# Attention scores of two heads in the two row halves of TensorE's array, three products instead of four, and two heads' queries turned by one transpose

## The chip, the cores and the metric

The kernel runs on one core of one Trainium2 chip, in one launch. The metric is the device time of the whole program in microseconds (us). Before the change it is 1516.78 us, the median of 3 runs (1512.79 to 1517.85).

## What is computed

One encoder layer over two sequences of 512 tokens with 1024 features: a state-space branch (S5) and a windowed attention branch, gated and merged, and then a squared-ReLU MLP. The change is in the attention branch. It has 16 query heads of 64 features, 4 key/value heads (so 4 query heads share one key head), blocks of 128 tokens, and each query block sees its own and its two neighbouring key blocks:

```python
q = rms_norm(q.reshape(bsz, seq_len, N_HEADS, HEAD_DIM), q_gain)
k = rms_norm(k.reshape(bsz, seq_len, N_KV_HEADS, HEAD_DIM), k_gain)
...
s = jnp.einsum('nqkgd,njkd->nkgqj', qb, kw).astype(jnp.float32) * scale + bias
s = jnp.where(mask[:, None, None], s, NEG_INF)
...
p = jax.nn.softmax(jnp.concatenate([s, sink_col], axis=-1), axis=-1)[..., :-1]
o = jnp.einsum('nkgqj,njkd->nqkgd', p.astype(vs.dtype), vw)
```

## The kernel before, in words

**Precision by parts.** Matmuls run in fp32r. To come near fp32, an operand is held as a high part (rounded to fp32r) and a low part (what the rounding left), and a product a*b is the sum of matmuls over the parts: high*high, high*low, low*high. In most places of this kernel that is three matmuls (`mm3`, L114 to L118).

**The attention stage** (in the trace about 418 to 692 us) goes through 8 steps: for each of the 4 key heads j, the two sequences sq. A step has 4 units, one for each query block qb of 128 tokens. A unit (class `Unit`, L805) treats the 4 query heads of its key head at once: scores (`scores`, L819), the bias and the row maximum on VectorE (`largest`, L825, printed as L827), the exponential on ScalarE (`exp`, L831), turning the probabilities on TensorE (`turn`, L836, printed L839), splitting them into parts (`high` on ScalarE L843, `low` on VectorE L848), the product with the values (`value`, L851, printed L855) and adding the two halves of the result (`lower_part` L859 on ScalarE, `add` L865 on VectorE). A unit with a middle query block has 3 key blocks (384 score columns), one at the end of a sequence 2 (256 columns): 16 units of each kind.

**Queries.** While a step's units run, the query projection of the next step is made, one block of 128 tokens in each unit (class `Tile`, L759): 24 matmuls of 256 columns (`project`, L772), squares and the norm factor (`square` on ScalarE, `power` on VectorE and GpSimd), scaling (`norm`, L789), four transposes, one for each head (`turn`, L794), and the split: the high part on ScalarE (`high`, L799) goes to partitions 0 to 63 and the low part on VectorE (`low`, L802) to partitions 64 to 127. So for each head the high part lies above the low part on the contraction axis. The keys lie twice, in both halves of the partitions (`key_copies`, `key_turn`), as a high tile `kh` and a low tile `kl`. One score matmul with all 128 rows against `kh` gives high*high + low*high, one against `kl` gives high*low + low*low: two matmuls a head, four products.

**The order.** In this stage the order of the instructions on TensorE, ScalarE, VectorE and GpSimd is written out by hand (`manual_schedule`, L973): the loop body L979 to L1073 is the order in each engine's queue, and each engine takes its queue in order. In one turn of the loop stand the scores and exponentials of the current unit `cur`, the turning, splitting and value products of the unit before it (`prev`), the final `add` of the one before that (`owed`), the projection of the next step's block (`new`), the turn and split of the block projected in the turn before (`rows`), pieces of weight to be split (`extra`: the cast on ScalarE when it is popped, the rest on VectorE when `lower()` is called), and once in a step the division by the sums (`div`, `late`) and the next step's keys. SyncE's queue is not written by hand here.

**PSUM.** Scores use the pool `ps_s` with 2 buffers of one bank, turned probabilities and keys `ps_t` with 2, projections and turned queries `ps_acc` with 3, the value product `ps_o` with 1.

**Another place that the prediction reads.** In the state-space part, `lags` (L453 to L462) writes two halves of PSUM's partitions with matmuls of a 64-column stationary operand, alternating between the halves:

```python
for e in range(2):
    gk = e * SH + g
    PE.matmul(ps[e * 64:(e + 1) * 64, g * 144:(g + 1) * 144], lbt[:, ri, q * SG + gk, :],
              ctab[:, gk, ri].rearrange("p n c -> p (n c)"),
              start=ri == 0, stop=ri == 1)
```

Of the kernel before, what the change touches and what calls it, by code (L numbers as in the profile page):

```python
# [12 lines left out]
F32 = mybir.dt.float32  # L13
F32R = mybir.dt.float32r
I32 = mybir.dt.int32
AF = mybir.ActivationFunctionType
# [3 lines left out]
P = 128  # L20
# [7 lines left out]
CB = 256  # L28
N_HEADS = 16
N_KV = 4  # L30
G = 4
# [32 lines left out]
def hybrid_layer(ctx, tc, x, rel, onehot, w_qkv, w_ug, vectors, lam, coefs, w_glu, w_out, ln2,  # L64
                 w_up, w_down, out):
    nc = tc.nc
    V, S, PE, GP, SP = nc.vector, nc.scalar, nc.tensor, nc.gpsimd, nc.sync
# [18 lines left out]
    def sps():  # L86
        return ps_s.tile([P, 512], F32, tag="sps", name="sps")
# [16 lines left out]
    ident = const.tile([P, P], F32, name="ident")  # L104
# [5 lines left out]
    bglu_sb, gain_q, gain_k, nsink = [vec[:, a:b] for a, b in ((0, 8), (8, 9), (9, 10), (10, 26))]  # L110
# [160 lines left out]
    with tc.tile_pool(name="xin", bufs=1, reuse_waits="tile") as xin, tc.tile_pool(name="ssmc", bufs=1) as sc:  # L271
# [146 lines left out]
        ps = ps_o.tile([P, 512], F32, tag="po", name="line")  # L418
# [276 lines left out]
    with tc.tile_pool(name="att", bufs=2, reuse_waits="tile") as ap, tc.tile_pool(name="attc", bufs=1, reuse_waits="tile") as ac:  # L695
# [63 lines left out]
        class Tile:  # L759
# [30 lines left out]

            def turn(self):
                self.pt = self.pt or acc()
                for h in range(G):
                    PE.transpose(self.pt[0:64, h * P:(h + 1) * P], self.qn[:, h], ident)  # L794

            def high(self):
                self.ptv = self.pt[0:64].rearrange("p (h t) -> p h t", h=G)
                self.dst = queries[self.key][:, :, self.t * P:(self.t + 1) * P]
                S.activation(self.dst[0:64], self.ptv, AF.Copy, scale=gain_q[0:64])  # L799

            def low(self):
                V.scalar_tensor_tensor(self.dst[64:128], self.ptv, gain_q[0:64], self.dst[0:64].bitcast(F32),  # L802
                                       op0=ALU.mult, op1=ALU.subtract)

        class Unit:  # L805
# [10 lines left out]
                self.nmx = small.tile([P, G], F32, tag="nmx", name="nmx")  # L816
                self.s, self.pt, self.hl = {}, {}, {}

            def scores(self, h):  # L819
                ps = self.s[h] = sps()  # L820
                qs = queries[self.j, self.sq][:, h, self.qb * P:(self.qb + 1) * P]
                for i, kk in enumerate(keys[self.j, self.sq]):
                    PE.matmul(ps[:, 0:self.nk], qs, kk[:, self.k0 * P:self.k1 * P], start=i == 0, stop=i == 1)  # L823

            def largest(self, h):  # L825
                hh, b0 = self.j * G + h, (self.k0 - self.qb + 1) * P
# [146 lines left out]
        with tc.manual_schedule(engines={ET.PE, ET.Activation, ET.DVE, ET.Pool}):  # L973
            for i, (j, sq) in enumerate(steps):
                nxt = steps[i + 1] if i + 1 < len(steps) else None
                sums = small.tile([P, G, NB], F32, tag="sm", name="sm", bufs=2)
                ya = ap.tile([P, 2, HALF], F32, tag="ya", name="ya")
                extra = pieces_of(i)
                for qb in range(NB):  # L979
                    if 1 <= i < 5:  # L980
                        e, t = divmod((i - 1) * NB + qb, T)
                        GP.dma_start(y2_scr[e, :, :, t, :].rearrange("g c k -> c g k"), y_scr[e, t])
                    if i == 7 and qb == 0:
                        load_gates(0)
                    for m in {6: (qb,), 7: ((4, 5), (6,), (7,), ())[qb]}.get(i, ()):
                        load_y(m)
                    cur = Unit(j, sq, qb, sums, ya)
                    n3 = prev.nkb if prev else 0
                    div = Divide(*steps[i - 1], *done) if qb == 1 and i > 0 else None
                    new = Tile(*nxt, qb) if nxt else None  # L990
                    project = new.project if new else lambda n: glu_pull(n // 2)
                    kd = None
                    if rows and not nxt:
                        rows.pt = acc()
                    if rows and not rows.qn:
                        rows.power()
                    cur.scores(0)
                    cur.largest(0)
                    if qb == 3 and late:
                        late.multiply()  # L1000
                    cur.scores(1)
                    if owed:
                        owed.add()
                    cur.largest(1)
                    if n3:
                        prev.turn(0)
                        prev.high(0)
                    project(6)
                    if n3:
                        prev.low(0)  # L1010
                    cur.exp(0)
                    cur.exp(1)
                    if rows and not rows.qn:
                        rows.norm()
                    if qb == 0 and nxt:
                        kd = key_copies(*nxt)
                    if div:
                        div.invert()
                    cur.scores(2)
                    cur.largest(2)  # L1020
                    if n3:
                        prev.turn(1)
                        prev.high(1)
                    project(4)
                    if n3:
                        prev.value(0, 0)
                    project(2)
                    cur.exp(2)
                    cur.scores(3)
                    if lower:  # L1030
                        lower()
                        lower = None
                    if n3:
                        prev.low(1)
                        prev.value(0, 1)
                    cur.largest(3)
                    if rows:
                        rows.turn()
                    if n3 > 2:
                        prev.turn(2)  # L1040
                    if kd:
                        key_turn(*nxt, kd)
                    if div:
                        div.turn()
                    project(4)
                    if rows:
                        rows.high()
                        rows.low()
                    if n3 > 2:
                        prev.high(2)  # L1050
                    if n3:
                        prev.value(1, 0)
                    cur.exp(3)
                    if n3 > 2:
                        prev.low(2)
                    project(4)
                    if n3:
                        prev.value(1, 1)
                    project(4)
                    if n3 > 2:  # L1060
                        prev.value(2, 0)
                        prev.value(2, 1)
                    if new:
                        new.square()
                    if n3:
                        prev.lower_part()
                    if extra:
                        lower = extra.pop(0)()
                    if qb == 1:
                        late = div  # L1070
                    owed, prev, rows = prev, cur, new
                    if nxt and qb == NB - 1 and sq == 1:
                        load_biases(nxt[0])  # L1073
                done = sums, ya
# [7 lines left out]
            for k in range(prev.nkb):  # L1082
                prev.value(k, 0)
                prev.value(k, 1)
            lower()
            prev.lower_part()
            prev.add()
            div = Divide(*steps[-1], *done, True)
# [461 lines left out]
```

## Time and profile before

| | |
|---|---|
| median of 3 runs | 1516.78 us (1512.79 to 1517.85) |
| the profiled execution | 1514.28 us, its span 1512.5 us |
| TensorE (PE) busy in the span | 96% |
| VectorE (DVE) busy | 74% |
| ScalarE (ACT) busy | 51% |
| mean granted TensorE clock | 0.992 |

The profile comes from one execution. PE is the matmul, PEld the weight load that belongs to it and overlaps the matmuls. Matmuls are pipelined: the duration of one (0.28 us for 256 columns) is longer than the distance at which the next one starts (0.12 us), so a share of busy time near 100% does not say that the array streams all the time. The rate is read from starts that follow each other. "L827" is line 827 of the kernel. In a row of instructions, `out<-in` gives the names of the tiles, `128*64` the rows and columns of the stationary operand, `128x256` the moving operand; in brackets or behind the last bar stands the idle time of the engine before them and what ended it.

### The profile page before, as it was taken

How to read it: one execution, taken by the hardware profiler on the slowest of the kernel's cores; microseconds unless marked ns; L12 is line 12 of the kernel's file. 1: busy time of each engine (PE TensorE's matmuls, PEld its weight loads, DVE VectorE, ACT ScalarE, POOL GpSimd, SP SyncE). 2: the span in 40 equal slices, each digit the busy share in tenths (PEclk: the TensorE clock that was granted, in tenths of full speed). 3: DMA queues.
4: the chain of work that ended last, by engine and by line, in shares of the span. 5: the costliest groups of instructions: out<-in, count | busy, mean ns of one | idle time of the engine just before them, and what ended most of it. 6: DMA issues, size and time to landing. Idle time of an engine off the chain costs nothing.

```text
span 1512.5 us, 21630 instructions
## 1 busy us (share of the span) xinstructions
PE 1458.2 (96%) x7818; PEld 1238.1 (82%) x7818; DVE 1117.1 (74%) x2015; ACT 764.8 (51%) x1362; POOL 192.2 (13%) x360
## 2 busy tenths in 40 slices
PE   6999999999999999997999989999999999999998
PEld 4788888878899998985787878888888888888787
DVE  7998859977646899886985468777777588575653
ACT  6777762235536787784343245555544443433332
POOL 3133351002231333220100000000000000000000
PEclk9999999999999999998999999999999999999999
DMA  4444459229831445273545235444443694454331
GB/s 172 139 167 166 159 168 368 106 86 348 298 124 32 144 120 161 90 276 119 204 170 176 91 112 174 153 151 151 152 153 125 243 359 150 153 181 153 123 123 62
DMA packets 102139, 249.65 MB, mean 165 GB/s; under 512 B 12266, under 2 KB 23786, under 8 KB 102032
## 3 DMA queue, kind: packets, MB, share of 16 engines
q1 hardware_dynamic: 58352, 135.88, 27.6%
q0 software_dynamic: 18048, 57.72, 11.1%
q10 hardware_dynamic: 25632, 54.67, 9.6%
q8 instruction: 62, 1.02, 0.3%
q14 instruction: 45, 0.37, 0.1%
HBM read 173.74 MB, written 90.21 MB: 175 GB/s over the span
## 4 chain that ended last, share of the span: by engine, by line
PE 78%; DVE 9%; ACT 4%; DMA 4%; issue 4%; POOL 1%; ACTq 0%; SPq 0%; DVEq 0%; POOLq 0%
PE acc L185 14%; PE bank L117 13%; PE bank L118 13%; PE bank L116 13%; PE acc L123 5%; PE acc L772 3%; PE acc L117 2%; PE acc L118 2%; PE acc L116 2%; PE po L855 2%; PE sps L547 2%; DVE pl L848 1%; PE sps L823 1%; PE tps L839 1%; DVE p L827 1%
## 5 line engine op out<-in xcount | busy, mean ns | idle before, releaser
L185 PE MATMUL acc<-act,c_hi 128*128 128x512 f32 x768 | 248.8, 399 | 1.0 <-DVE act L304 1.0
L117 PE MATMUL bank<-b_lo,a_hi 128*128 128x512 f32 x448 | 174.5, 390 | 1.1 <-DVE b_lo L1419 1.1
L118 PE MATMUL bank<-b_hi,a_lo 128*128 128x512 f32 x448 | 174.3, 389 | 0.0
L116 PE MATMUL bank<-b_hi,a_hi 128*128 128x512 f32 x448 | 173.5, 389 | 0.0
L185 PEld LDWEIGHTS acc<-act,c_hi 128*128 128x128 f32 x768 | 142.0, 189 | 29.8 <-DVE act L304 2.4
L185 PE MATMUL acc<-act,c_lo 128*128 128x512 f32 x384 | 152.3, 397 | 0.0
L1418 ACT CAST a_hi<-d_a 128x1024 fp32r<-128x1024 f32 x56 | 59.0, 1054 | 179.1 <-PE bank L117 175.7
L116 PE MATMUL bank<-act,act 128*128 128x512 f32 x368 | 144.3, 392 | 4.9 <-ACT act L1308 4.9
L118 PE MATMUL bank<-act,act 128*128 128x512 f32 x368 | 144.2, 392 | 0.0
L117 PE MATMUL bank<-act,act 128*128 128x512 f32 x368 | 144.1, 392 | 0.0
L1419 DVE TENSOR_TENSOR a_lo<-d_a,a_hi 128x1024 fp32r<-128x1024 f32 x56 | 68.5, 1223 | 100.2 <-ACT a_hi L1418 100.2
L772 PE MATMUL acc<-w_hi,act 128*128 128x256 f32 x512 | 116.2, 295 | 0.0
L117 PEld LDWEIGHTS bank<-b_lo,a_hi 128*128 128x128 f32 x448 | 84.1, 188 | 19.3 <-DVE b_lo L1419 1.9
L118 PEld LDWEIGHTS bank<-b_hi,a_lo 128*128 128x128 f32 x448 | 84.1, 188 | 17.5
L116 PEld LDWEIGHTS bank<-b_hi,a_hi 128*128 128x128 f32 x448 | 84.1, 188 | 17.3
L123 PE MATMUL acc<-act,gc_hi 128*128 128x512 f32 x256 | 84.3, 408 | 13.3 <-ACT ga L1133 10.7
L772 PEld LDWEIGHTS acc<-w_hi,act 128*128 128x128 f32 x512 | 87.0, 189 | 3.7
L116 PEld LDWEIGHTS bank<-act,act 128*128 128x128 f32 x368 | 69.8, 190 | 19.8 <-ACT act L1308 5.3
L185 PEld LDWEIGHTS acc<-act,c_lo 128*128 128x128 f32 x384 | 72.4, 189 | 14.1 <-DVE c_lo L176 0.5
L833 ACT ACTIVATE p<-p,nmx 128x257 f32<-128x257 f32 (+1 forms) x128 | 72.2, 564 | 21.9 <-DVE nmx L827 20.3
L118 PEld LDWEIGHTS bank<-act,act 128*128 128x128 f32 x368 | 69.6, 189 | 14.9 <-DVE act L1309 0.4
L117 PEld LDWEIGHTS bank<-act,act 128*128 128x128 f32 x368 | 69.7, 189 | 14.4
(327 smaller groups left out, 3440.3 us busy)
## 6 DMA issues: line engine op xcount, KB each, us to landing
d_a<-a_scr SPq DMA_DIRECT2D x56, 512.0 KB, 3.6
u_raw<-in_w_up_dram SPq DMA_DIRECT2D x32, 512.0 KB, 5.1
a_scr<-t ACTq DMA_DIRECT2D x64, 256.0 KB, 4.9
k<-in_w_down_dram SPq DMA_DIRECT2D x32, 512.0 KB, 6.0
c_raw<-in_w_ug_dram SPq DMA_DIRECT2D x48, 256.0 KB, 3.7
a_scr<-a ACTq DMA_DIRECT2D x46, 256.0 KB, 2.0
ct_scr<-ctab POOLq DMA_DIRECT2D x16, 576.0 KB, 3.5
ctab_in<-ct_scr POOLq DMA_DIRECT2D x16, 576.0 KB, 7.6
```

The costliest lines, as they stand in the source:

```text
L116: PE.matmul(ps, a[0], b[0], start=first, stop=False)
L117: PE.matmul(ps, a[0], b[1], start=False, stop=False)
L118: PE.matmul(ps, a[1], b[0], start=False, stop=last)
L123: PE.matmul(ps, w[wi][:, k, :], rows[yi], start=k + p == 0, stop=k == KT - 1 and p == 2)
L185: PE.matmul(ps, w[wi][:, k, :], hT[s][hi][:, k, :], start=n == 0, stop=n == 3 * KT - 1)
L547: PE.matmul(ps[:, i * P:(i + 1) * P], bm[:, ri, g, :], u_sb[:, gp * SH + g, :], start=True, stop=True)
L772: PE.matmul(self.ps, hT[sq][act][:, k, col:col + P], w[:, k % 4, :], start=i == 0, stop=i == 3 * KT - 1)
L823: PE.matmul(ps[:, 0:self.nk], qs, kk[:, self.k0 * P:self.k1 * P], start=i == 0, stop=i == 1)
L833: S.activation(p, p, AF.Exp, bias=self.nmx[:, h:h + 1], scale=-1.0, accum_out=self.sums[:, h, self.qb:self.qb + 1])
L855: PE.matmul(self.po, vv, self.hl[i][part], start=i + part == 0, stop=i == self.nkb - 1 and part == 1)
L1418: S.copy(hi, src)
L1419: V.tensor_sub(lo, src, hi.bitcast(F32))
```

## The change

Three things are changed together.

- `Tile.turn` makes two transposes of 128 x 128 instead of four of 128 x 64: two heads stand above each other after the turn. `high` and `low` then work on 128 partitions x 256 elements instead of 64 x 512. In the tile of queries the first index is now the part (high or low) and the pair m of heads, and the partitions hold the two heads of a pair.
- `Unit.scores` takes a pair of heads. Each head has the 64 rows of its half of the array, and three products are made (high*high, high*low, low*high; low*low is left out): 6 matmuls of 64 rows for two heads, alternating between the halves, into the two score banks. Before, there were 4 matmuls of 128 rows for two heads.
- The order of the unit is rewritten: the scores stand at two places of a unit instead of four, the projection goes in pieces of 8, 4, 4, 4 and 4 instead of 6, 4, 2, 4, 4 and 4, and `exp(2)`, `low(1)`, `low(2)`, `rows.low()`, the cast of a weight piece and its `lower()` move.

```diff
             def turn(self):
                 self.pt = self.pt or acc()
-                for h in range(G):
-                    PE.transpose(self.pt[0:64, h * P:(h + 1) * P], self.qn[:, h], ident)
+                for m in range(2):
+                    PE.transpose(self.pt[:, m * P:(m + 1) * P],
+                                 self.qn[:, 2 * m:2 * m + 2].rearrange("p e d -> p (e d)"), ident)
 
             def high(self):
-                self.ptv = self.pt[0:64].rearrange("p (h t) -> p h t", h=G)
-                self.dst = queries[self.key][:, :, self.t * P:(self.t + 1) * P]
-                S.activation(self.dst[0:64], self.ptv, AF.Copy, scale=gain_q[0:64])
+                self.ptv = self.pt[:, 0:CB].rearrange("p (m t) -> p m t", m=2)
+                self.dst = [queries[self.key][:, n * 2:n * 2 + 2, self.t * P:(self.t + 1) * P] for n in range(2)]
+                S.activation(self.dst[0], self.ptv, AF.Copy, scale=gain_q)
 
             def low(self):
-                V.scalar_tensor_tensor(self.dst[64:128], self.ptv, gain_q[0:64], self.dst[0:64].bitcast(F32),
+                V.scalar_tensor_tensor(self.dst[1], self.ptv, gain_q, self.dst[0].bitcast(F32),
                                        op0=ALU.mult, op1=ALU.subtract)
...
-            def scores(self, h):
-                ps = self.s[h] = sps()
-                qs = queries[self.j, self.sq][:, h, self.qb * P:(self.qb + 1) * P]
-                for i, kk in enumerate(keys[self.j, self.sq]):
-                    PE.matmul(ps[:, 0:self.nk], qs, kk[:, self.k0 * P:self.k1 * P], start=i == 0, stop=i == 1)
+            def scores(self, m):
+                self.s[2 * m], self.s[2 * m + 1] = sps(), sps()
+                qs = queries[self.j, self.sq][:, :, self.qb * P:(self.qb + 1) * P]
+                for n, (a, b) in enumerate(((0, 0), (0, 1), (1, 0))):
+                    for e in range(2):
+                        rows = slice(e * 64, (e + 1) * 64)
+                        PE.matmul(self.s[2 * m + e][:, 0:self.nk], qs[rows, a * 2 + m],
+                                  keys[self.j, self.sq][b][rows, self.k0 * P:self.k1 * P], start=n == 0, stop=n == 2)
...
                     cur.largest(0)
                     if qb == 3 and late:
                         late.multiply()
-                    cur.scores(1)
+                    cur.largest(1)
                     if owed:
                         owed.add()
-                    cur.largest(1)
                     if n3:
                         prev.turn(0)
                         prev.high(0)
-                    project(6)
+                    project(8)
                     if n3:
                         prev.low(0)
                     cur.exp(0)
...
-                    cur.scores(2)
-                    cur.largest(2)
                     if n3:
                         prev.turn(1)
                         prev.high(1)
+                    if extra:
+                        lower = extra.pop(0)()
                     project(4)
                     if n3:
                         prev.value(0, 0)
-                    project(2)
-                    cur.exp(2)
-                    cur.scores(3)
-                    if lower:
-                        lower()
-                        lower = None
+                    cur.scores(1)
+                    cur.largest(2)
                     if n3:
-                        prev.low(1)
                         prev.value(0, 1)
-                    cur.largest(3)
                     if rows:
                         rows.turn()
                     if n3 > 2:
...
+                    cur.largest(3)
                     project(4)
                     if rows:
                         rows.high()
-                        rows.low()
+                    if n3:
+                        prev.low(1)
                     if n3 > 2:
                         prev.high(2)
+                        prev.low(2)
+                    if rows:
+                        rows.low()
                     if n3:
                         prev.value(1, 0)
+                    cur.exp(2)
                     cur.exp(3)
-                    if n3 > 2:
-                        prev.low(2)
                     project(4)
...
                     if n3:
                         prev.lower_part()
-                    if extra:
-                        lower = extra.pop(0)()
+                    if lower:
+                        lower()
+                        lower = None
```

After the loop, one `lower()` that was left over goes.

More of the change, by code (lines that the diff above doesn't have):

```diff
@@ L1084, in hybrid_layer @@
                 prev.value(k, 1)
-            lower()
             prev.lower_part()
```

## The prediction

> **What bounds the kernel now.** I read the page first, for the whole program.
>
> ```profile
> PE 1458.2 (96%) x7818; PEld 1238.1 (82%) x7818; DVE 1117.1 (74%) x2015; ACT 764.8 (51%) x1362; POOL 192.2 (13%) x360
> ```
>
> TensorE carries the program; the other engines have room on the average. That average says little about one stage, so next I took the busy time by stretches: the four lead-in tiles and the values' projection, then the loop with the units.
>
> ```profile
> core 0: us, PE busy (x) PEld busy (x) DVE busy (x) ACT busy (x) POOL busy (x), PEclk, DMA share, GB/s
> 415.00:465.00 50.00, 48.31 (x403) 47.90 (x402) 18.67 (x39) 13.61 (x30) 13.17 (x22) 1.00 0.28 98
> 465.00:692.00 227.00, 222.45 (x1596) 203.78 (x1595) 201.02 (x518) 179.19 (x453) 59.84 (x111) 1.00 0.45 143
> ```
>
> In the loop (227 us, 32 units, 7.1 us each, full clock) VectorE is busy 201 us, almost as much as TensorE. So I need TensorE's own stream without its waits. The groups of TensorE by form in 465 to 692 us give the counts:
>
> ```profile
> L772 PE MATMUL acc<-w_hi,act 128*128 128x256 f32 x448 | 104.0, 297 | 0.0
> L772 PE MATMUL acc<-w_lo,act 128*128 128x256 f32 x224 | 63.0, 281 | 0.0
> L839 PE MATMUL tps<-ident,p 128*128 128x128 f32 x312 | 46.7, 272 | 0.0
> L855 PE MATMUL po<-pl,va 128*128 128x512 f32 x77 | 32.9, 427 | 3.7 <-DVE pl L848 3.0
> L855 PE MATMUL po<-ph,va 128*128 128x512 f32 x77 | 31.0, 403 | 0.5 <-DVE ya L865 0.3
> L823 PE MATMUL sps<-kh,qa 128*128 128x384 f32 x64 | 21.7, 340 | 0.3 <-DVE nmx L827 0.3
> L823 PE MATMUL sps<-kl,qa 128*128 128x384 f32 x64 | 21.6, 338 | 0.0
> L794 PE MATMUL acc<-ident,qn 128*64 128x128 f32 x116 | 17.5, 273 | 0.0
> L823 PE MATMUL sps<-kl,qa 128*128 128x256 f32 x64 | 17.4, 282 | 0.0
> L823 PE MATMUL sps<-kh,qa 128*128 128x256 f32 x64 | 17.3, 281 | 0.0
> L123 PE MATMUL acc<-act,gc_hi 128*128 128x512 f32 x31 | 11.3, 427 | 0.0
> ```
>
> Their mean durations are latencies; what one costs in a stream is the distance from start to start, from TensorE's timeline (two stretches of the loop; first the start in us, then the length):
>
> ```profile
> 505.55 0.34 PE L823 MATMUL sps<-kh,qa 128*128 128x384 f32 x1
> 505.73 0.34 PE L823 MATMUL sps<-kl,qa 128*128 128x384 f32 x1
> 505.90 0.34 PE L823 MATMUL sps<-kh,qa 128*128 128x384 f32 x1
> 506.07 0.33 PE L823 MATMUL sps<-kl,qa 128*128 128x384 f32 x1
> 506.25 0.60 PE L839 MATMUL tps<-ident,p 128*128 128x128 f32 x4
> ...
> 521.51 0.28 PE L823 MATMUL sps<-kh,qa 128*128 128x256 f32 x1
> 521.63 0.28 PE L823 MATMUL sps<-kl,qa 128*128 128x256 f32 x1
> ```
>
> A third stretch, from the state-space part, has 512 columns (L185), and between them the matmuls of `lags` (L459), to which I come back:
>
> ```profile
> 66.62 0.61 PE L185 MATMUL acc<-act,c_hi 128*128 128x512 f32 x2
> 67.08 0.39 PE L185 MATMUL acc<-act,c_lo 128*128 128x512 f32 x1
> 67.39 1.20 PE L459 MATMUL lag<-ctab,lbt 128*64 128x144 f32 x16
> 68.42 1.15 PE L459 MATMUL sps<-ctab,lbt 128*64 128x144 f32 x16
> 69.50 0.73 PE L185 MATMUL acc<-act,c_hi 128*128 128x512 f32 x2
> 70.08 0.39 PE L185 MATMUL acc<-act,c_lo 128*128 128x512 f32 x1
> ```
>
> 384 columns cost (506.25 - 505.55)/4 = 0.175 us, 256 columns 0.12. Four transposes span 0.60 at 0.272 each, so one follows another after (0.60 - 0.272)/3 = 0.109. 512 columns cost (67.08 - 66.62)/2 = 0.23. The stream is then 672 x 0.12 (L772) + 312 x 0.109 (L839) + 154 x 0.23 (L855) + 128 x 0.175 + 128 x 0.12 (L823) + 116 x 0.109 (L794) + 31 x 0.23 (L123) = 207 us, and some 8 us of smaller groups that I do not list: 215 of 227 us, 6.7 us a unit. TensorE bounds the loop, and some 12 us are stalls. What ends most of them is in the waits of its weight loads in the same window (us in total, times, the longest):
>
> ```profile
> PEld po L855 <- DVE pl L848: 9.0, 21, 0.8
> ```
>
> The value product waits for VectorE's low part. A piece of VectorE's timeline in a unit with three key blocks shows why:
>
> ```profile
> 506.60 0.61 DVE L827 CUSTOM_DVE_ANT_0 p<-sps,bias,vec 128x384 f32<-128x384 f32 x1
> ...
> 511.87 0.74 DVE L802 SCALAR_TENSOR_TENSOR qa<-acc,vec,qa 64x512 fp32r<-64x512 f32 x1
> 512.64 0.69 DVE L848 TENSOR_TENSOR pl<-tps,ph 128x512 fp32r<-128x512 f32 x1
> ```
>
> From the first maximum to the end of the last `pl` VectorE needs 6.7 us in its queue, and `rows.low()` (0.74) stands ahead of that `pl`.
>
> **The change part by part.** *Transposes of queries:* two of 0.109 go in each of 32 tiles (28 in the loop, 4 in the lead-in, where TensorE is busy 48.3 of 50 us): -7.0 us, all on TensorE's stream.
>
> *Split of queries:* the same elements lie in 128 partitions x 256 instead of 64 x 512.
>
> ```profile
> L789 DVE TENSOR_TENSOR qn<-acc,rq 128x256 f32<-128x256 f32 x28 | 11.6, 413 | 0.0
> ```
>
> By L789's 0.413 (the nearest row of that size, also read from PSUM) `low` falls from 0.74 by 0.33: VectorE -9 us over 28 units, to about 192. `high` on ScalarE gets shorter likewise. Neither is on TensorE's stream; they count through the stalls.
>
> *Scores:* a pair of heads had 4 matmuls, and gets 6 of 64 rows in 3 pairs. No row shows matmuls in two row halves. The nearest shows two column halves, `lags` at L459, between full matmuls of L185, in the third stretch above. One fp32 matmul of 144 columns alone would cost 0.109 x 144/128 = 0.123, and 32 of them 3.9 us; the 32 took from 67.39 to 69.50, 2.1 us. So two halves run side by side, the weight loads too, and a pair costs one. For the scores I take the same: 3 x 0.175 instead of 4 x 0.175 for the 32 pairs of heads with 384 columns (-5.6 us), 3 x 0.12 instead of 4 x 0.12 for the 32 with 256 (-3.8): -9.4 us. The other bound is two halves one after the other, 6 streams for 4: +18.9.
>
> *Going in and out of the halves.* From 67.08 to 70.08 stand 3.00 us. Three full matmuls are 0.69 and 16 pairs of 0.123 are 1.97. The rest, 0.34 us, is what one excursion costs: a gap of 0.08 before the first half, about 0.1 before the first full matmul, and weight loads that could not be made ahead. There are two excursions a unit, 64 in all: with this price +21.8 us. The bounds are 0 and 0.34 (a gain is out, since every change of shape in these rows costs something or nothing); nothing in the trace shows row halves, and I take 0.34 because it is the only change of shape of this kind that the trace has. The Trainium skill has a rule that speaks against the change here, "TensorEngine Tiling (Array Packing)", section Key Properties: a change of the tiling mode, unlike a change between tiles of one mode, drains the engine. By it the row halves pay as the column halves do; were it true of column halves alone, the sum would be 21.8 us lower. The trace agrees for columns (the 0.34), and no run here shows it for rows.
>
> *Stalls.* Scores at two places need both banks of `ps_s` at once: `scores(1)` waits for `largest(0)` and `largest(1)`. TensorE has until then turn(0), project(8), turn(1), project(4) and one value product, 4 x 0.109 + 8 x 0.12 + 4 x 0.109 + 4 x 0.12 + 0.23 = 2.5 us; VectorE needs two L827 of at most 0.61 plus small reads. That wait is covered. The cast of a weight piece moves ahead by half a unit, with `rows.high`, `high(2)` and the exponentials behind it in ScalarE's queue; its load is on SyncE, whose queue the change does not touch, and its buffer comes free with the `lower()` two pieces back, more than a unit before.
>
> ```profile
> L730 ACT CAST w_hi<-w_raw 128x512 fp32r<-128x512 f32 x12 | 7.4, 619 | 0.0
> ```
>
> Twelve casts waited for nothing before, and half a unit (3.5 us) is little against the 7.1 us that lie between two pieces, so I take none; if a load should be late, ScalarE's tail (below) is what it costs. The waits on `pl` get shorter: ahead of the last `low` no longer stand `rows.low()` (0.74) and the `lower()` of a weight piece, so it lands 0.7 us or more earlier in VectorE's queue; the longest of the old waits was 0.8. `lower()` now stands at the unit's end, with `power` and the next `largest` queued behind it, and scores of the next unit need only the two maxima already done. With the excursions TensorE has (215 - 9.4 - 6.1 + 21.8)/32 = 6.9 us a unit, VectorE 192/32 = 6.0: slack 0.9 instead of 0.4. I take 8 of the 12 us of stalls as gone; the bounds are 0 and 12.
>
> *Sum*, against the profiled execution (1514.28 us, 1.8 over its span, and 2.5 under the median of the runs): 1514.3 - 7.0 - 9.4 + 21.8 - 8.0 = 1511.7 us. A difference of 0.3%, 4.5 us, is about what a measurement of this kernel can tell from no change; this sum is 2.6 below and so within it.
>
> **The rivals.** *Cheap excursions.* Row halves may need less than the 0.34: the trace's row is for column halves in fp32 and a stationary operand of 64 columns, the scores are row halves in fp32r with 128. At 0 the stream is (215 - 15.5)/32 = 6.2 a unit, hardly above VectorE's 6.0, so no stall goes: 1497.9. At 0.17 it is 10.9 us of excursions and perhaps 3 us of stalls gone: 1505.8. Middle 1502. For it: nothing measured; against it: the one row.
>
> *Halves that do not overlap* (the change does not do what it says). Then 64 groups cost 6 streams: 1514.3 - 7.0 + 18.9 = 1526.2 without excursions, and with them and some 10 us of stalls gone 1538. It decides if the second matmul of a pair starts a stream (0.12 or 0.175) after the first. Against it: L459 ran two at a time. For it: in L459 the halves write different partitions, here two matmuls write the same partitions of two banks.
>
> *ScalarE's tail.* `exp(2)` and `exp(3)` now come after the last `high`, and `square` and `lower_part` behind them.
>
> ```profile
> L843 ACT CAST ph<-tps 128x512 fp32r<-128x512 f32 x78 | 44.9, 575 | 5.4 <-PE tps L839 4.8
> L833 ACT ACTIVATE p<-p,nmx 128x385 f32<-128x385 f32 x64 | 39.6, 618 | 9.4 <-DVE nmx L827 8.1
> ...
> L778 ACT ACTIVATE sq<-acc 128x256 f32<-128x256 f32 x28 | 10.6, 380 | 6.5 <-PE acc L772 5.8
> ```
>
> `rows.high` (by L778's size 0.38), `high(2)` 0.575, two exponentials of 0.618 and `square` 0.38 are 2.6 us. They can begin when `rows.turn` is out, 0.7 us after `scores(1)` (0.23 of a value product, two transposes, 0.27 until the last is in), and end 3.3 after it. TensorE has 5 value products, 6 transposes and 12 projections until the next scores, 1.15 + 0.65 + 1.44 = 3.2. `power` at the head of VectorE's next turn waits for `square`, with the next `largest` behind it. So the two are even, and a delay of 0.3 (half an L827 ahead of `exp(3)`) would be paid in 28 units: +8.4, 1520.1. Against it: VectorE's slack of 0.9 above, which can take the delay up.
>
> **How the numbers follow.** Forecast 0.44, cheap excursions 0.31, halves one after the other 0.11, ScalarE's tail 0.14. The forecast's own range is 1507.7 (all stalls gone) to 1519.7 (none gone). Faster by over 0.3% (below 1509.7): all of the cheap excursions and 0.13 of the forecast, 0.44. Slower (above 1518.9): 0.11, 0.11 of the tail, 0.05 of the forecast, 0.27. Within: 0.29. The range 1499 to 1524 leaves out the cheapest excursions and the serial halves, together less than 0.2.
>
> **What would show it.** The two matmuls of a pair at L823's successor should start within 0.01 us of each other, and three pairs of 384 columns take 0.53. The first full matmul behind a group should start some 0.2 us late and the group's first some 0.1; if both gaps are missing, the cheap case is right. The waits on `pl` should fall from 9.0 to about 3. L794 should count 56 in the loop, VectorE's busy time there fall to about 192 us. I am wrong if the pair's starts lie 0.12 apart, if VectorE waits on `square` in most units, or if the loop's length leaves 217 to 230 us.

## The result and the profile after

The changed kernel takes 1531.22 us (median of 4 runs, 1527.91 to 1533.02) against 1516.51 before (4 runs): a ratio of 1.0101, 95% interval 1.0083 to 1.0119. It is slower by 14.7 us, above the range of the forecast (1499 to 1524). The profiled executions differ by 1526.1 - 1512.5 = 13.6 us of span.

The time came in the attention loop: from the first score matmul of its first unit to that of its last lie 220.5 us before (465.4 to 685.8) and 234.3 after (463.8 to 698.1), 13.8 more. Its busy times, over a stretch that is 13 us longer than before's because the loop is:

```profile
core 0: us, PE busy (x) PEld busy (x) DVE busy (x) ACT busy (x) POOL busy (x), PEclk, DMA share, GB/s
465.00:705.00 240.00, 227.10 (x1654) 187.23 (x1653) 194.13 (x518) 170.92 (x453) 59.49 (x111) 1.00 0.42 136
```

VectorE fell from 201 to 194 us and ScalarE from 179 to 171, as the split on all 128 partitions should do; the clock is full. The split itself, `low` on VectorE and `high` on ScalarE, which took 0.745 and 0.672 us before:

```profile
L803 DVE SCALAR_TENSOR_TENSOR qa<-acc,vec,qa 128x256 fp32r<-128x256 f32 x29 | 13.8, 476 | 0.0
```

```profile
L800 ACT ACTIVATE qa<-acc,vec 128x256 fp32r<-128x256 f32 x29 | 13.6, 470 | 19.1 <-PE acc L794 19.1
```

So the engines have less to do and the loop is longer.

The scores, first. The groups of TensorE in the loop (window 465 to 710 us), and then its timeline around one group of a unit with two key blocks:

```profile
L826 PE MATMUL sps<-kh,qa 64*128 64x384 f32 x128 | 25.4, 386 | 0.8 <-DVE nmx L831 0.8
L826 PE MATMUL sps<-kh,qa 64*128 64x256 f32 x124 | 19.2, 329 | 0.0
...
L794 PE MATMUL acc<-ident,qn 128*128 128x128 f32 x58 | 11.1, 273 | 0.0
```

```profile
525.62 0.40 PE L859 MATMUL po<-ph,va 128*128 128x512 f32 x1
525.95 0.39 PE L826 MATMUL sps<-kh,qa 64*128 64x256 f32 x2
526.18 0.28 PE L826 MATMUL sps<-kl,qa 64*128 64x256 f32 x2
526.29 0.28 PE L826 MATMUL sps<-kh,qa 64*128 64x256 f32 x2
526.50 0.50 PE L859 MATMUL po<-pl,va 128*128 128x512 f32 x1
526.84 0.38 PE L794 MATMUL acc<-ident,qn 128*128 128x128 f32 x2
```

The stationary operand is now 64*128: row halves. Each row holds a pair (x2) in the time of one matmul: from the second pair to the third it is 0.11 to 0.12 us, the distance of full matmuls of 256 columns before. And the excursion is there. The value product at 525.62 streams 0.23, so the next matmul could start at 525.85; the first pair starts at 525.95 (0.10 late), the second 0.23 after it instead of 0.12 (0.11 late), the third pair's stream ends at 526.41 and the next full matmul starts at 526.50 (0.09 late), and the one behind it 0.34 later instead of 0.23 (0.11 late): 0.41 us. Where four transposes follow, the last term is smaller and the sum 0.35. The weight loads show the same from their side; in the loop they now stand idle before the scores 47 times, while the profile shows nothing that they wait for:

```profile
PEld sps L826 <- issue: 13.9, 47, 0.4
```

Then the waits of TensorE's matmuls in the loop (window 465 to 707 us): us in total, times and the longest.

```profile
PE po L859 <- DVE pl L852: 8.5, 7, 1.4
PE po L859 <- DVE ya L869: 3.7, 7, 0.5
```

Six of the seven waits for a low part are of 1.38 to 1.39 us, each in the first unit of a step; the seventh is of 0.16. The place, in TensorE's timeline and in VectorE's:

```profile
528.56 0.28 PE L772 MATMUL acc<-w_lo,act 128*128 128x256 f32 x1
530.23 0.51 PE L859 MATMUL po<-pl,va 128*128 128x512 f32 x1 [1.38 <-DVE pl L852]
```

```profile
527.02 0.08 DVE L831 DVE_READ_ACCUMULATOR2_ANT nmx<- 128x1 f32 x1
528.42 0.75 DVE L756 SCALAR_TENSOR_TENSOR kl<-tps,vec,kh 128x512 fp32r<-128x512 f32 x1 [1.32 <-ACT kh L755]
529.09 0.47 DVE L831 CUSTOM_DVE_ANT_0 p<-sps,bias,vec 128x256 f32<-128x256 f32 x1
529.49 0.08 DVE L831 DVE_READ_ACCUMULATOR2_ANT nmx<- 128x1 f32 x1
529.49 0.68 DVE L852 TENSOR_TENSOR pl<-tps,ph 128x512 fp32r<-128x512 f32 x1
```

This is the first unit of a step, in which the next step's keys are turned. VectorE stands idle for 1.32 us at `kl` (L756), which needs ScalarE's `kh`; behind `kl` in its queue are `largest(3)` and `low(1)`, whose result TensorE needs at once. In the old order VectorE waited for `kh` at this place too (6.6 us in seven times, against 9.5 now), but `low(1)` and `largest(3)` stood ahead of `key_turn`.

### The profile page after: what moved, and what is told of

The parts are those of the page before. It is cut to its first block, busy times and chain, and to the rows that moved or that the text cites. A ratio compares the mean times of both kernels' runs of the same rounds, so it can differ in the third digit from the quotient of the medians.

```text
span 1526.1 us, 21733 instructions
## 1 busy us (share of the span) xinstructions
PE 1464.3 (96%) x7882; PEld 1222.7 (80%) x7882; DVE 1109.6 (73%) x2015; ACT 755.2 (49%) x1362; POOL 192.6 (13%) x360
## 4 chain that ended last, share of the span: by engine, by line
PE 83%; DVE 6%; ACT 4%; DMA 4%; issue 3%; POOL 1%; ACTq 0%; SPq 0%; DVEq 0%; POOLq 0%
PE acc L185 13%; PE bank L117 13%; PE bank L118 13%; PE bank L116 13%; PE acc L772 5%; PE acc L123 4%; PE po L859 3%; PE sps L826 3%; PE acc L117 2%; PE acc L118 2%; PE acc L116 2%; PE tps L843 2%; PE sps L547 2%; DMA w_raw<-in_w_out_dram 1%; DMA toep<-toep_scr 1%
## 5 line engine op out<-in xcount | busy, mean ns | idle before, releaser
L772 PE MATMUL acc<-w_hi,act 128*128 128x256 f32 x512 | 111.8, 296 | 0.0
L831 DVE CUSTOM_DVE_ANT_0 p<-sps,bias,vec 128x256 f32<-128x256 f32 (+1 forms) x128 | 66.3, 548 | 17.8 <-PE sps L826 17.3
```

Of the source, the lines that this page charges most:

```text
L772: PE.matmul(self.ps, hT[sq][act][:, k, col:col + P], w[:, k % 4, :], start=i == 0, stop=i == 3 * KT - 1)
L831: V.tensor_tensor_reduce(self.p[:, h, 1:1 + self.nk], self.s[h][:, 0:self.nk], biases[self.j][h][:, b0:b0 + self.nk], -1.0, nsink[:, hh:hh ...
```

## The experiments

The theory after the result (A): the excursions cost what the forecast took, and a new wait in the first unit of a step brings some 11 us. Its rivals: the excursions cost much more and carry it all (B); scores of two heads at one place starve VectorE, whatever the order (C).

The table reads each run's trace: the distance from one unit's first score matmul to the next unit's, mean over the steps, for the four units of a step (units 1 and 4 have two key blocks). Each ratio is against the kernel before, run beside it.

| run | unit 1 | unit 2 | unit 3 | unit 4 | us, median | ratio (95%) |
|---|---|---|---|---|---|---|
| before | 6.20 | 6.64 | 7.96 | 7.72 | 1516.51 | |
| the change | 7.73 | 7.11 | 7.55 | 7.88 | 1531.22 | 1.0101 (1.0083 to 1.0119) |
| e1_low1_ahead | 6.49 | 6.99 | 7.55 | 7.88 | 1520.27 | 1.0018 (1.0009 to 1.0028) |
| e2_old_order | 7.03 | 7.56 | 8.46 | 9.91 | 1552.97 | 1.0234 (1.0219 to 1.0249) |
| e3_twice_out | 8.57 | 7.93 | 8.41 | 8.68 | 1557.45 | 1.0264 (1.0249 to 1.0279) |
| e4_order_alone | 7.45 | 6.78 | 7.47 | 7.58 | 1521.86 | 1.0032 (1.0022 to 1.0042) |
| e5_pair_turn | 5.98 | 6.93 | 8.45 | 8.15 | 1522.94 | 1.0050 (1.0033 to 1.0067) |
| e6_order_low1 | 6.21 | 7.07 | 7.47 | 7.59 | 1516.81 | 1.0000 (0.9989 to 1.0011) |
| e7_order_pair_turn | 6.26 | 7.39 | 7.83 | 8.10 | 1522.93 | 1.0056 (1.0035 to 1.0078) |
| e8_multiply_later | 7.11 | 7.39 | 7.83 | 7.11 | 1524.45 | 1.0051 (1.0035 to 1.0067) |
| e9_one_excursion | 6.19 | 7.05 | 7.55 | 7.92 | 1518.93 | 1.0011 (1.0001 to 1.0021) |
| e10_gp_multiply | 6.26 | 7.06 | 7.55 | 6.94 | 1510.53 | 0.9963 (0.9948 to 0.9978) |
| e11_before_gp | 6.20 | 6.64 | 7.96 | 6.96 | 1511.18 | 0.9965 (0.9953 to 0.9977) |
| e12_mended_gp | 6.49 | 6.99 | 7.55 | 7.24 | 1514.21 | 0.9991 (0.9982 to 1.0000) |

### The low part ahead of the keys

On the changed kernel:

```diff
+                    cur.largest(3)
+                    if n3:
+                        prev.low(1)
                     if kd:
                         key_turn(*nxt, kd)
                     if div:
                         div.turn()
-                    cur.largest(3)
                     project(4)
                     if rows:
                         rows.high()
-                    if n3:
-                        prev.low(1)
```

> The changed kernel with one step of VectorE's queue moved: largest(3) and prev.low(1) stand ahead of the next step's key_turn, whose low part kl (L756) waits for ScalarE's kh. Only the first unit of a step is touched. Theory A (64 excursions at 0.34 to 0.40 us, and a new wait in the first unit of a step, where low(1) stands behind kl, about 1.5 us in 7 units): 10 to 12 us faster than the changed kernel, 1519 to 1522, some 0.3% over before. Theory B (the excursions alone cost more than that and carry the whole 14.7 us; the wait is only a shadow of them): no change, 1529 to 1532.

Measured: 1520.27 us, 10.9 under the changed kernel. Unit 1 fell from 7.73 to 6.49 and no other unit by more than 0.12. As A has it, and against B: about three quarters of the loss stood in one place of VectorE's queue. The edit moves `largest(3)` together with `low(1)`, and no run has one without the other; the wait on TensorE that went is the one for `low(1)`. Of the waits of TensorE's matmuls one kind is left:

```profile
PE po L859 <- DVE ya L869: 3.6, 7, 0.5
```

### The new scores in the old order

The changed kernel's queries and scores in the loop of the kernel before; against that loop:

```diff
                     cur.scores(0)
...
-                    cur.scores(1)
...
-                    cur.scores(2)
+                    cur.scores(1)
...
-                    cur.scores(3)
```

> The kernel before with the new queries and the new scores, in the old order (the pair's scores where the first and the third head's scores stood). Theory A: stream -9.4 - 7.0 + 22 to 24, stalls as before or up to 8 us fewer: -2 to +8 against before, 1514 to 1525. Theory B: about the changed kernel's time, 1529 to 1533. Theory C (scores of a pair need both score banks at once, and VectorE starves between them, whatever the order): 1529 or more.

Measured: 1552.97 us, 36 over before and far over what A and B said. TensorE's weight loads (first row) and matmuls (second) wait for the maxima, and the timeline shows one such wait:

```profile
PEld sps L826 <- DVE nmx L831: 25.1, 30, 1.6
```

```profile
PE sps L826 <- DVE nmx L831: 18.4, 29, 1.4
```

```profile
543.01 0.44 PE L826 MATMUL sps<-kh,qa 64*128 64x384 f32 x1
544.00 0.44 PE L826 MATMUL sps<-kh,qa 64*128 64x384 f32 x1 [0.55 <-DVE nmx L831]
544.00 0.60 PE L826 MATMUL sps<-kl,qa 64*128 64x384 f32 x2
```

One half starts and the other waits a microsecond for its bank: `ps_s` has two, and the second pair needs both emptied by `largest`, which in the old order stand late in VectorE's queue. C is right for the old order, and not "whatever the order": in the rewritten one the change has a single such wait on TensorE, of 0.75 us. A's figure was wrong. Scores by pairs needed an order rewritten for them.

### Twice as many excursions

`scores` of the changed kernel, with `project` handed in:

```diff
                         PE.matmul(self.s[2 * m + e][:, 0:self.nk], qs[rows, a * 2 + m],
                                   keys[self.j, self.sq][b][rows, self.k0 * P:self.k1 * P], start=n == 0, stop=n == 2)
+                    if n == 0:
+                        between(2)
```

> The changed kernel with twice as many excursions: after the first pair of each group the projection gives two full matmuls (taken from its last pieces), so the array goes into the row halves and out of them twice in each group, 128 times instead of 64. The same instructions otherwise. Theory A: 64 x 0.34 to 0.40, +22 to +26 us over the changed kernel, 1553 to 1557. Theory B: an excursion costs 0.5 or more, +32 us or more. If excursions were cheap or hidden: +0 to +8.

Measured: 1557.45 us, 26.2 over the changed kernel, 0.41 for each of the 64 further excursions. A group with two full matmuls in its middle:

```profile
541.78 0.45 PE L826 MATMUL sps<-kh,qa 64*128 64x384 f32 x2
542.15 0.39 PE L772 MATMUL acc<-w_hi,act 128*128 128x256 f32 x1
542.38 0.28 PE L772 MATMUL acc<-w_lo,act 128*128 128x256 f32 x1
542.59 0.44 PE L826 MATMUL sps<-kl,qa 64*128 64x384 f32 x2
542.87 0.34 PE L826 MATMUL sps<-kh,qa 64*128 64x384 f32 x2
```

From 541.78 to 542.59 are 0.81 us for a pair and two matmuls that stream 0.175 + 0.24; the other 0.40 is going out of the halves and in again. That is A's upper end (the time lies 0.45 us over its range), and under B's 0.5. In each of the four units the price is the same: they are longer by 0.80 to 0.86 us for two excursions.

### The order alone

The changed kernel with `Tile.turn`, `high` and `low` as before and

```diff
+            def scores(self, m):
+                for h in (2 * m, 2 * m + 1):
+                    self.head(h)
+
+            def head(self, h):
+                ps = self.s[h] = sps()
+                qs = queries[self.j, self.sq][:, h, self.qb * P:(self.qb + 1) * P]
+                for i, kk in enumerate(keys[self.j, self.sq]):
+                    PE.matmul(ps[:, 0:self.nk], qs, kk[:, self.k0 * P:self.k1 * P], start=i == 0, stop=i == 1)
```

so that `head` is the old `scores`.

> The new order with the old queries and the old scores (four products, full array; a pair's scores at one place): no excursions, none of the two savings. Theory A: the wait in the first unit of a step stays, about 1.5 us in 7 units, and nothing else is added: +8 to +12 over before, 1524 to 1529. Theory B: the order costs nothing, 1514 to 1518. Theory C: the two places for scores cost by themselves, as much as A or more, and not in the first unit of a step alone.

Measured: 1521.86 us, 5.0 over before. The wait in unit 1 is there without any row halves:

```profile
PE po L859 <- DVE pl L852: 8.3, 6, 1.4
```

Unit 1 is 1.25 longer than before; unit 3 is 0.49 shorter, a gain that A's figure had left out, so the time lies under A's range and over B's. In the kernel before, six value products waited 0.5 us for the last `low` of unit 3, and those waits are gone:

```profile
PE po L855 <- DVE pl L848: 3.0, 6, 0.5
```

So the order carries the new wait, and gives part of it back where the last `low` no longer stands behind `rows.low()`.

### The order alone, mended

The edit of the first experiment on the run above.

> The new order alone (old queries, old scores) with largest(3) and prev.low(1) ahead of key_turn, as in the first experiment. Theory A (the new order is good but for that one place): 1.5 us in 7 units go from the order alone, so 1510 to 1512, 5 to 7 us under before. Then the difference between this and the changed kernel with the same mending is what row halves, three products and the new turn cost together: -9.4 - 7.0 + 64 excursions. Rival (the wait hides another that comes next): 1516 to 1522.

Measured: 1516.81 us, ratio 1.0000, not the 5 to 7 us less that A expected. The wait on `pl` is gone, and others come up:

```profile
PE po L859 <- DVE ya L869: 3.3, 7, 0.5
PE po L859 <- ACT p L837: 2.0, 5, 0.4
```

Unit 1 came back to 6.21, but unit 2, where the waits for `p` lie, rose from 6.78 to 7.07 (before: 6.64) and eats what unit 3 gained. The rival is right: the mended order is worth nothing by itself. Against it the mended change (1.0018) has the new turn, three products and the excursions: by the two medians 3.5 us more, by the two ratios 2.7.

### Two transposes without row halves

On the kernel before. Head 2m keeps high above low, head 2m + 1 has low above high, so one score matmul still covers both:

```diff
+                for m in range(2):
+                    PE.transpose(self.pt[:, m * P:(m + 1) * P],
+                                 self.qn[:, 2 * m:2 * m + 2].rearrange("p e d -> p (e d)"), ident)
...
+                for e in range(2):
+                    r = slice(e * 64, (e + 1) * 64)
+                    S.activation(self.dst[r, :, e], self.ptv[r], AF.Copy, scale=gain_q[r])
...
+                for e in range(2):
+                    r, o = slice(e * 64, (e + 1) * 64), slice((1 - e) * 64, (2 - e) * 64)
+                    V.scalar_tensor_tensor(self.dst[o, :, e], self.ptv[r], gain_q[r], self.dst[r, :, e].bitcast(F32),
+                                           op0=ALU.mult, op1=ALU.subtract)
```

> The kernel before, old order and old scores, with only the two transposes for two heads: the split then writes high and low of a pair so that each head still has its high part in one half of the partitions and its low part in the other (two instructions of 64 x 256 on ScalarE and two on VectorE instead of one of 64 x 512 on each). Theory A (TensorE's stream sets the time, a transpose costs 0.109): -7.0 us if the stalls stay, -3 to -7 since VectorE gets some 0.1 us a unit more: 1510 to 1514. Rival (in the old order VectorE sets the pace in half of the units, so what TensorE saves is waited for): -2 to +2.

Measured: 1522.94 us, 7 over before, though TensorE has 7 us less to do. The split's instructions on VectorE and on ScalarE:

```profile
L807 DVE SCALAR_TENSOR_TENSOR qa<-acc,vec,qa 64x256 fp32r<-64x256 f32 x58 | 28.0, 483 | 6.3 <-ACT qa L802 4.7
```

```profile
L802 ACT ACTIVATE qa<-acc,vec 64x256 fp32r<-64x256 f32 x58 | 26.9, 463 | 0.5
```

Two of 0.483 for one of 0.745, and two of 0.463 for one of 0.672: 0.22 and 0.25 us a unit more on two engines. Unit 1 got shorter by 0.22, as much as two transposes cost in TensorE's stream; units 2 to 4 got longer by 0.29, 0.49 and 0.43. Both expectations missed. TensorE does not set the pace in those three units alone; a little more on the other two engines costs more than TensorE saved. Which of the two it is, no run separates.

### The same on the mended order, and the multiply moved

Two transposes and four split instructions on the mended order:

> The mended new order with the two transposes for two heads, scores on the full array as before. Theory A: the run before it minus 4 to 7 us, 1504 to 1508; against the mended changed kernel it lacks only the row halves, so the difference is 64 excursions minus 9.4: 12 to 16 us. Rival (the split's four instructions cost VectorE and ScalarE what TensorE saves): the same as the order alone.

Measured: 1522.93 us, 1.0056: 6 us over the mended order, about as in the old one. Both expectations missed here too. The mended change with its row halves is 2.7 us faster than this run, not 12 to 16 slower, because this run pays for the split in four instructions. Then with the multiply behind `rows.low()`:

```diff
-                    if qb == 3 and late:
-                        late.multiply()
...
                     if rows:
                         rows.low()
+                    if qb == 3 and late:
+                        late.multiply()
```

> As the run before it, with late.multiply() (1.2 us of VectorE in the last unit of a step, ahead of owed.add and low(0)) moved behind rows.low(). It stood ahead of the add for which the value product waited 0.5 us in 7 units. If that wait is on the path: 3 to 4 us less. Rival (the multiply then delays the next unit's maxima instead): the same or slower.

Measured: 1524.45 us, no change that the intervals can tell. Unit 4 fell by 0.99 and the unit after it, unit 1, rose by 0.85: the 1.2 us were only carried over, as the rival said.

### One excursion where the banks allow it

The mended change. With two key blocks a bank holds the scores of two heads, so both pairs go at one place:

```diff
+                wide = self.nkb > 2
+                if not wide and m == 1:
+                    return
+                pairs = (m,) if wide else (0, 1)
+                banks = sps(), sps()
...
+                for i, m in enumerate(pairs):
+                    for e in range(2):
+                        self.s[2 * m + e] = banks[e][:, i * CB:i * CB + self.nk]
```

> The mended changed kernel of the first experiment, with one excursion instead of two in the units with two key blocks: there both pairs of heads have their scores in two banks (heads 0 and 2 in one, 1 and 3 in the other), 12 matmuls one after the other at the place of scores(0). 16 of 64 excursions go, nothing else. Theory A (each excursion is 0.34 to 0.40 us of TensorE's time on the path): -5.4 to -6.4 against the mended kernel, 1514 to 1515. Rival (in the first and last unit of a step VectorE and ScalarE set the pace, and what TensorE saves there is waited for): 0 to -2, 1518 to 1520.

Measured: 1518.93 us (1.0011), 1.3 under the mended change by the medians, and the intervals overlap. The units tell more: unit 1 fell by 0.30, most of an excursion's price, and unit 4 not at all (7.88, 7.92). In unit 4 something else sets the pace, as the rival said for both units.

### The multiply on GpSimd, on three kernels

```diff
-                V.tensor_mul(self.ya, self.ya, self.fac)
+                (V if self.last else GP).tensor_tensor(self.ya, self.ya, self.fac, op=ALU.mult)
```

On the run above, on the kernel before, and on the mended change:

> As the run before it, and late.multiply() (1.2 us on VectorE in the last unit of a step, with owed.add, low(0) and the value product behind it) on GpSimd, which is busy a quarter of this stage. If VectorE's queue is what the last unit of a step waits for: 4 to 8 us less (7 times 0.5 to 1.2 us). Rival (GpSimd and VectorE slow each other, or the next unit only waits elsewhere): 0 to +4.

> The kernel before with the multiply of the steps but the last on GpSimd, as a control for the run above. If the old order too waits for VectorE in the last unit: 4 to 8 us under before, 1508 to 1512. If TensorE's stream alone sets its pace: 1515 to 1517.

> The mended changed kernel (two excursions in every unit) with the multiply on GpSimd: against the run with one excursion in the units with two key blocks and the same multiply it has 16 excursions more, now with VectorE relieved. Theory A (an excursion is 0.34 to 0.40 us of TensorE's time, and is paid where TensorE sets the pace): 3 to 6 us over that run, 1513 to 1517. Rival (those units are still paced by VectorE or ScalarE): 0 to 2 over it, 1510 to 1513.

Measured: 1510.53, 1511.18 and 1514.21 us. In all three unit 4 gets shorter by 0.6 to 1.0 us and the other units stay within 0.07. GpSimd takes about twice as long for it as VectorE did (1.22 us in the old trace), and has the time; its row in the first of the three:

```profile
L904 POOL TENSOR_TENSOR ya<-ya,fac 128x1024 f32<-128x1024 f32 x7 | 16.7, 2391 | 13.3 <-DMA fac<-rs_scr 13.3
```

So VectorE's queue set the pace of unit 4, in the old order as in the new. With it relieved the excursion counts there too: between the last run and the first, unit 4 differs by 0.30 and unit 1 by 0.23, and the times by 3.7 us, in A's 3 to 6. The two fastest, the kernel before with this one line and the reworked change with it, are both faster than before and not to be told from each other.

## Why the prediction was wrong

- *Transposes of queries.* Right: 58 in the loop instead of 116, at 273 ns, none of them waiting. (The prediction said 56; the last tile of the lead-in is turned in the loop.) That their going shortens the loop was shown for unit 1 alone, in the run with two transposes without row halves.
- *Split.* Right in kind, and less than taken: `low` fell from 0.745 to 0.476, not 0.413.
- *Scores.* Right: two halves start together, and three pairs cost three streams. The measured time lies between the two figures of the rival of halves one after the other (1526.2 and 1538), but that is chance: its mechanism is out.
- *Excursions.* Right in kind, and a little too small. The column halves of L459 gave 0.34; the row halves show 0.35 and 0.41 in the timeline, and 0.41 by the doubled excursions. At 0.38 they are 24 us instead of 21.8. The rule of the Trainium skill ("TensorEngine Tiling (Array Packing)", Key Properties: a change of mode drains) now has a row here for row halves as well. The rival of cheap excursions is out.
- *Stalls.* This is the step that failed: "I take 8 of the 12 us of stalls as gone". They grew. From the first unit's first score matmul to the last unit's, the time can be sorted into the stream (0.109, 0.119, 0.175 or 0.232 us for each matmul of 128, 256, 384 or 512 columns, a pair counted once), the excursions (what lies over the stream from the matmul ahead of a group of scores to the second one behind it) and the rest, the stalls. Summed over all starts in the trace, in us, each rounded by itself and as exact as those distances, so to about 1 us:

| run | stream | excursions | stalls | together |
|---|---|---|---|---|
| before | 208.6 | 0 | 11.8 | 220.5 |
| the change | 193.2 | 23.6 | 17.6 | 234.3 |
| e1_low1_ahead | 193.2 | 23.4 | 6.9 | 223.4 |
| e6_order_low1 | 208.6 | 0 | 10.5 | 219.1 |
| e11_before_gp | 208.6 | 0 | 6.5 | 215.1 |
| e12_mended_gp | 193.2 | 22.9 | 2.8 | 218.9 |

The 11.8 us of stalls, which the prediction had sized rightly, became 17.6 instead of 4. The prediction followed the last `low` of a unit, which did move to the front, and the weights' `lower()`, and not `low(1)`, which the change moves behind `key_turn`. There `kl` waits in VectorE's queue for ScalarE's `kh`, and behind it `low(1)` and a value product: 10.9 us by the first experiment. The waits of TensorE's weight loads on `pl` were to fall from 9.0 to 3; the change has the first row, and the second with the place mended:

```profile
PEld po L859 <- DVE pl L852: 10.8, 10, 1.6
```

```profile
PEld po L859 <- DVE pl L852: 1.5, 5, 0.6
```

The rest of the step was too large as well: with the place mended 6.9 us of stalls are left, so 4.9 went, not 8, and the mended order with the old queries and scores takes only 1.3 of them (e6_order_low1). What the prediction said of the score banks held: `scores(1)` hardly waits for them in the new order.

- *TensorE bounds the loop.* Too simple. By its own stream (215 of 227 us) it did, on the average of the units. In unit 4 VectorE did: saved time on TensorE was waited for there (one excursion less, unit 4 unchanged), and 1.2 us taken from VectorE shortened that unit by 0.8 in the kernel before. In the table, the multiply on GpSimd takes 5.3 us of stalls from the kernel before and 4.1 from the mended change.
- *ScalarE's tail.* Two of the prediction's signs of being wrong came: the loop's length, and VectorE's wait for `square`, in 25 of the 28 units that have one. The two rows are of before and of the change:

```profile
DVE ms L782 <- ACT sq L778: 5.6, 15, 0.9
```

```profile
DVE ms L782 <- ACT sq L778: 15.7, 25, 1.1
```

The wait stands at 12.3 us in the mended change, and in the mended change with the multiply on GpSimd too, where all stalls of TensorE together are 2.8. So little of it lies on the path, and this rival does not carry the loss.

In one line, for the loop: 15.4 us less stream, 23.6 for going in and out of the halves and 5.8 more stalls (10.7 for one place in a queue, 4.9 fewer elsewhere) make 14.0, of which the distances from unit to unit show 13.8; the whole program became 14.7 us slower.

## What to carry to other kernels

Narrow matmuls packed into halves of the array pay only if one excursion carries enough of them: here each excursion saved 0.12 to 0.175 us (one stream of four) and cost 0.35 to 0.41. When an order is rewritten by hand, follow each moved instruction past every instruction that it now stands behind, and ask what that one waits for: VectorE's wait for `kh` cost little while `low(1)` stood ahead of it, and stalled TensorE as well once that needed result was put behind it. Where three engines are busy by 79 to 98% of a stage, read the bound unit by unit, not stage by stage.

## What the runs showed of the hardware

Row halves ran two at a time at the full rate, though both wrote the same partitions, in two banks: one pair followed another after 0.11 to 0.12 us at 256 columns. Going in and out cost 0.35 to 0.41 us, a little more than the 0.34 of the column halves of L459.

A stationary operand of 64 columns did not cost this by itself. The kernel before has another row of that shape, which the prediction did not weigh as a change of shape, the four transposes of queries between full matmuls:

```profile
509.47 0.40 PE L855 MATMUL po<-pl,va 128*128 128x512 f32 x1
509.71 0.60 PE L794 MATMUL acc<-ident,qn 128*64 128x128 f32 x4
510.14 0.60 PE L839 MATMUL tps<-ident,p 128*128 128x128 f32 x4
510.50 0.37 PE L772 MATMUL acc<-w_hi,act 128*128 128x256 f32 x1
510.70 0.28 PE L772 MATMUL acc<-w_lo,act 128*128 128x256 f32 x1
```

From 509.47 to 510.70 are 1.23 us, and the streams alone make 0.232 + 8 x 0.109 + 0.119 = 1.22. So the change removed no excursion together with these transposes. Unlike L459 they all write the same half of the partitions; whether that is what makes the difference, no run shows.

On VectorE and ScalarE the split of 64 x 256 took as long (0.483 and 0.463) as that of 128 x 256 in the changed kernel (0.476 and 0.470), and 64 x 512 took 0.745 and 0.672: here more partitions cost nothing, and more elements in each did. By the two sizes of 64 partitions each instruction brings some 0.22 and 0.25 us of its own, an estimate. A multiply of 128 x 1024 took 2.39 us on GpSimd and 1.22 on VectorE.
